# Neighbourhood attention on one core: the order, the loads and the sends of the closing projection

## The chip, the cores and the metric

The kernel runs on one core of one Trainium2 chip. The metric is the device time of one execution in microseconds. Three executions of the kernel before took 1041.56, 1041.59 and 1039.85 us; their median, 1041.56 us, is the number that the change is measured against.

## What is computed

One encoder layer (DEPTH is 1) with neighbourhood attention over 2048 tokens of width 1024, 16 heads of width 64, all in float32:

```python
h = rmsnorm(x, norm_0)
q, k, v, gate = jnp.split(h @ w_in_0, 4, axis=-1)
o = neighbourhood_attention(heads(q), heads(k), heads(v), rpb_0)
x = x + (o * jax.nn.silu(gate)) @ w_out_0
return rmsnorm(x, norm_f)
```

The change touches the last two lines alone: the product with `w_out_0` (1024 by 1024), the addition of the rows of `x`, the final norm, and when the operands of these arrive.

## The kernel before, in words

**Stages.** `stage_one` and `stage_two` compute q, k, v and the gate. Then a loop of 33 steps (m = 0 to 32) runs the attention, one pair of heads and one quarter T of the tokens a step: scores (L972), the bias added from a table tile `em` (L981), exponentials, transposes (`turns`, L1015), and the product with the values (`values`, L1034), whose result is multiplied by the gate tile `sgt` (L1038, tile `og`) and stored to DRAM as `ogd`. Between these parts `feed(n)` weaves in n matmuls of other work, first the remaining values, then `outputs()` (L1229 to L1233), which is the output projection of the first 1024 tokens. In the first half of the tokens the projection is a plain product; a finished row is stored by L1142.

**The end stretch.** The second 1024 tokens are projected by `tail()`, after the loop. They form four units n = 0 to 3 of 256 tokens. Each unit is a 2 by 2 block product done with seven block products P = 1 to 7 (a Strassen form) in place of eight. A product is 12 matmuls (L1304): 4 slices of the inner dimension, each with three matmuls, because every float32 operand is split into a high and a low part. Left operands are the four blocks A11, A12 (loaded by `load_a`, L1267), A21, A22 (`load_b`, L1276), or the sums S1 to S4 of them (`sum_a`, VectorE, L1289); each is split by `form_a` into the two parts, ScalarE first (L436), then VectorE (L437), into a tile `f`. Right operands are three blocks of the weights, which lie in SBUF, and four combinations T1 to T4, which stage two had formed and stored to DRAM as `wodT`; each has 4 slices of 2 parts, so 32 loads of 256 KB in all bring them back (`load_w`, L1416).

**Which product waits for which.** The products of one unit share three PSUM banks: P 1 and 2 one, P 6, 7 and 4 the second, P 5 and 3 the third. A bank keeps accumulating: `evac_o` reads it after P 6 (L1371, L1372: U2 = bank + U1, then added to the row), and only then may P 7 add to it; it is read again after 7 (L1375, L1376) before 4 may go on. L1362 and L1363 belong to P 2, L1379 to P 5, L1383 to P 4, L1389 to P 3. After P 4 and after P 3 a row block is complete: ScalarE squares it (L1315), VectorE and ScalarE make the root (L1321 to L1323), VectorE scales both halves (L1328), and `send` stores them (L1332). The very last block has its own code, `last_row` (from L1343 on), with its two stores at L1354.

**What sets the order.** `order_t` is the order of the 28 products, written by hand. Every other instruction of the end stretch is put in a list with a due time counted in matmuls (`at`, `store`), and `due` emits what has come due after each matmul. Emission fixes the order inside each engine and inside each queue: an instruction that waits holds all behind it on its engine. All loads and all but one store go out on one queue, SyncE's (SP). Forms come due 23 matmuls before their product, the root of a row 6 matmuls after its last addition, its scaling 12 and its send 24 after.

**Tiles.** `get2` hands out 128 by 512 tiles: the free list `free2` first, else a new tile from a pool named by the list `grow`. A new tile takes the slot whose content is the oldest of its pool, and its first writer waits until that content has been read; for `raw` these are finished rows of the first half, waiting for L1142. `places` lists the slots for the combinations, made of tiles that the attention no longer needs.

Of the kernel before, what the change touches and what calls it, by code (L numbers as in the profile page):

```python
# [60 lines left out]
def build(ctx, tc, x, xr, xt, wg, tab, w_out, n0, nf, out):  # L61
# [1188 lines left out]
    def get2():  # L1250
        if not free2:
            return grow.pop(0)([128, 512], F32, "t2")
        return free2.pop(0)
# [3 lines left out]
    order_t = [(0, 1), (1, 1), (0, 2), (1, 2), (2, 1),  # L1257
# [4 lines left out]

# [54 lines left out]
    def finish_o(n, a):  # L1317
# [12 lines left out]
        def send():  # L1330
            for c in range(2):
                nc.sync.dma_start(out[row(n, a):row(n, a) + 128, 512 * c:512 * c + 512], R[n, a, c])  # L1332
                free2.append(R[n, a, c])
# [22 lines left out]
    def evac_o(n, P):  # L1356
# [16 lines left out]
        elif P == 7:  # L1373
            U[n, 3] = U[n, 2]
            nc.vector.tensor_tensor(U[n, 3], p, U[n, 1], OP.add)  # L1375
            nc.vector.tensor_tensor(R[n, 1, 1], R[n, 1, 1], U[n, 3], OP.add)  # L1376
            free2.append(U[n, 1])
        elif P == 5:
            nc.vector.tensor_tensor(R[n, 1, 1], p, R[n, 1, 1], OP.add)  # L1379
            square_o(n, 1, 1)  # L1380
            free2.append(U[n, 3])
        elif P == 4:
            nc.vector.tensor_tensor(R[n, 1, 0], p, R[n, 1, 0], OP.add)  # L1383
            square_o(n, 1, 0)
            finish_o(n, 1)
        elif (n, P) == (3, 3):
            last_row()
        else:
            nc.vector.tensor_tensor(R[n, 0, 1], p, R[n, 0, 1], OP.add)  # L1389
            square_o(n, 0, 1)  # L1390
            finish_o(n, 0)

    def before_end(m):
        if m == cycles - 1:
            load_b(0, [ep([128, 512], F32, "og2") for _ in range(2)])
            load_a(0, wp([128, 1024], F32, "og4"))

    def tail():
        for k in range(4):
            for f, q, j in (("B11", k, 0), ("B21", 4 + k, 0), ("B22", 4 + k, 1)):  # L1400
                WO[f, k] = woh[q, j], wol[q, j]
        load_a(1, wp([128, 1024], F32, "og4"))
        places = places_of([(emp, 4), (kp, 2), (emp, 4), (kp, 2)] + sixths() + [(vp, 2)] * 2 + [(mkp, 3)])
        places = list(places) + [qp([128, 512], F32R, "tw") for _ in range(2)] + [xp([128, 512], F32R, "tw") for _ in range(7)]
        grow.extend([sp] * 2 + [raw] * 4 + [ev] * 4 + [rbp] * 3 + [ev] * 2 + [raw] * 2 + [xp, lp])
        base = 576 - fed[0]
        slots_ = {u: base + 12 * i for i, u in enumerate(order_t)}

        def at(t, f, *a):
            store(("tail",), t, lambda: f(*a))  # L1410

        def load_w(f, k):
            WO[f, k] = places.pop(0), places.pop(0)
            must(*[("wo", k, f, m) for m in range(2)])
            for m in range(2):
                nc.sync.dma_start(WO[f, k][m].bitcast(F32), wod[f][:, k, m])  # L1416

# [5 lines left out]
        for n in range(4):  # L1423
# [3 lines left out]
            if n > 1:  # L1427
                at(14 if n == 2 else base + 72, load_a, n)
            if n:
# [5 lines left out]
            for P in range(1, 8):  # L1435
                at(max(at_[P] - 23, 1), form_and_free, n, P)
        for f, t in (("T2", 1), ("T3", 20), ("T1", 36), ("T4", 52)):
            for k in range(4):
                at(t + 3 * k, load_w, f, k)
        while next(outs, 0) != 0:  # L1440
            due(1)
        for n, P in order_t:
# [63 lines left out]
    for m in range(cycles + 1):  # L1506
        a = amount[m] - 6
        begin(m)
        feed(6)
        if m:  # L1510
# [3 lines left out]
        if m:  # L1514
            for k in range(4):
                if not split_rows() and k % 2:
                    consume(1, turn=True)
                feed(a * (0.17, 0.17, 0.17, 0.19)[k])
# [53 lines left out]
```

## Time and profile before

| | us |
|---|---|
| median of three executions | 1041.56 |
| the profiled execution's own time | 1039.36 |
| its span | 1037.6 |
| TensorE busy in the span | 1010.8 (97%) |
| VectorE, ScalarE, GpSimd busy | 708.9, 517.7, 161.6 |
| last matmul of the first half's projection starts | 930.60 |
| first matmul of the end stretch starts | 930.83 |
| last matmul of the end stretch starts | 1028.87 |

All times of the trace are counted from the start of the span. A row of the timeline gives start, duration, engine, line, operation, `out<-in` and shape; what stands in brackets is how long the engine stood idle before the row and what released it. "PEclk" is the granted share of TensorE's clock.

### The profile page before, as it was taken

What the parts mean: (1) busy time and instruction counts of PE and PEld (TensorE: products, weight loads), DVE (VectorE), ACT (ScalarE), POOL (GpSimd) and SP (SyncE); (2) the same over time, 40 slices, a digit from 0 to 9 for tenths busy, and PEclk for the clock granted to TensorE, in tenths of its full rate; (3) what the DMA queues carried; (4) which work ended last, traced back from release to release, by engine and by line L of the source; (5) the groups of instructions that cost most, each with busy time, mean ns of one, the idle gap of its engine ahead of it and who ended that gap; (6) DMA issues with size and microseconds to landing.
All of it is one profiled execution on the core that took longest, in us unless ns stands there. A gap on an engine that the chain in (4) does not pass through costs nothing.

```text
span 1037.6 us, 21699 instructions
## 1 busy us (share of the span) xinstructions
PE 1010.8 (97%) x8128; PEld 813.4 (78%) x8128; DVE 708.9 (68%) x1569; ACT 517.7 (50%) x1301; POOL 161.6 (16%) x277
## 2 busy tenths in 40 slices
PE   9999999999999999999999999999999999996896
PEld 6888888887888888888888877777777777785774
DVE  5476657678897896767675656667667676653775
ACT  7645323244234443424333357787777776742333
POOL 0000231221221400000000022232332322310000
PEclk9999999999999999999999999999999999998899
DMA  9633444452735344665753798999888989879322
GB/s 318 230 102 102 142 144 134 129 160 85 202 102 183 99 136 156 219 195 165 218 178 111 239 271 284 317 338 316 267 279 267 312 292 329 295 232 391 124 99 82
DMA packets 125442, 213.84 MB, mean 206 GB/s; under 512 B 11352, under 2 KB 45528, under 8 KB 125336
## 3 DMA queue, kind: packets, MB, share of 16 engines
q1 hardware_dynamic: 124904, 212.05, 63.5%
q8 instruction: 64, 1.05, 0.4%
q10 hardware_dynamic: 432, 0.40, 0.1%
q14 instruction: 42, 0.34, 0.1%
HBM read 153.69 MB, written 58.72 MB: 205 GB/s over the span
## 4 chain that ended last, share of the span: by engine, by line
PE 81%; DVE 9%; DMA 3%; ACT 3%; issue 2%; SPq 1%; POOL 0%; DVEq 0%; ACTq 0%
PE pp L354 41%; PE pv L478 8%; PE o L1034 7%; PE s L972 6%; PE pv L871 4%; PE ph L1015 4%; PE po L1233 3%; PE po L1229 3%; PE po L1231 3%; PE pt L1304 2%; DMA kt<-kd 1%; DVE f L437 1%; DVE l L437 1%; DMA out_dram<-y 1%; DVE t L1328 1%
## 5 line engine op out<-in xcount | busy, mean ns | idle before, releaser
L354 PE MATMUL pp<-h,f 128*128 128x512 f32 x768 | 248.4, 389 | 0.0
L354 PEld LDWEIGHTS pp<-h,f 128*128 128x128 f32 x768 | 144.2, 188 | 29.8
L354 PE MATMUL pp<-four,f 128*128 128x512 f32 x648 | 160.8, 389 | 0.4 <-DVE u L367 0.3
L354 PE MATMUL pp<-l,f 128*128 128x512 f32 x384 | 149.4, 389 | 0.0
L354 PEld LDWEIGHTS pp<-four,f 128*128 128x128 f32 x648 | 121.4, 188 | 26.5 <-DVE u L367 1.4
L986 ACT ACTIVATE x<-x,st 128x264 f32<-128x264 f32 (+1 forms) x256 | 124.4, 487 | 23.8 <-DVE st L981 23.8
L998 POOL TENSOR_SCALAR x<-x,st 128x264 f32<-128x264 f32 (+1 forms) x192 | 86.9, 470 | 236.7 <-DVE st L991 236.0
L374 POOL TENSOR_TENSOR tmp<-tmp,rb 128x512 f32<-128x512 f32 x36 | 59.2, 1647 | 268.1 <-DVE tmp L372 223.4
L981 DVE CUSTOM_DVE_ANT_0 x<-s,em 128x264 f32<-128x264 f32 (+1 forms) x256 | 89.5, 404 | 2.0 <-PE s L972 1.8
L1034 PEld LDWEIGHTS o<-pta,vt 120*64 120x64 f32 (+2 forms) x1024 | 68.5, 137 | 19.8 <-DVE st L981 12.2
L354 PEld LDWEIGHTS pp<-l,f 128*128 128x128 f32 x384 | 72.1, 188 | 15.0
L1034 PE MATMUL o<-pta,vt 120*64 120x192 f32 (+5 forms) x1024 | 83.4, 316 | 0.0
L1018 DVE COPY pta<-ph 120x512 f32<-120x512 f32 (+5 forms) x96 | 56.0, 637 | 39.4 <-PE ph L1015 39.3
L362 ACT ACTIVATE p<-pp 128x512 f32<-128x512 f32 x24 | 14.3, 597 | 122.6 <-PE pp L354 122.6
L437 DVE TENSOR_TENSOR f<-raw,f 128x512 fp32r<-128x512 f32 x80 | 55.0, 690 | 27.1 <-ACT f L436 27.1
L1018 ACT ACTIVATE pta<-ph 120x512 f32<-120x512 f32 (+5 forms) x96 | 49.1, 557 | 41.7 <-PE ph L1015 41.7
L972 PE MATMUL s<-kt,qt 64*32 64x264 f32 (+1 forms) x2048 | 67.1, 374 | 0.6 <-DVE pta L1018 0.4
L436 ACT ACTIVATE f<-raw 128x512 fp32r<-128x512 f32 x80 | 49.5, 625 | 32.3 <-PE pp L354 16.6
L478 PE MATMUL pv<-wh,h 128*128 128x512 f32 x192 | 63.7, 392 | 0.4 <-ACT h L439 0.4
L478 PE MATMUL pv<-wl,h 128*128 128x512 f32 x192 | 63.4, 390 | 0.0
L478 PE MATMUL pv<-wh,l 128*128 128x512 f32 x192 | 63.2, 389 | 0.0
L372 DVE TENSOR_TENSOR tmp<-pp,u 128x512 f32<-128x512 f32 x48 | 33.1, 689 | 40.1 <-PE pp L354 35.4
(207 smaller groups left out, 1770.9 us busy)
## 6 DMA issues: line engine op xcount, KB each, us to landing
raw<-in_wg_dram SPq DMA_DIRECT2D x124, 256.0 KB, 4.3
em<-in_tab_dram SPq DMA_DIRECT2D x16, 912.0 KB, 7.5
em<-in_tab_dram SPq DMA_DIRECT2D x16, 528.0 KB, 7.4
vd<-v SPq DMA_DIRECT2D x32, 256.0 KB, 2.7
sgd<-sg SPq DMA_DIRECT2D x32, 256.0 KB, 3.7
qt<-qd SPq DMA_DIRECT2D x32, 256.0 KB, 5.7
sgt<-sgd SPq DMA_DIRECT2D x32, 256.0 KB, 8.4
ogd<-og SPq DMA_DIRECT2D x32, 256.0 KB, 3.8
```

Source lines behind the costliest of these rows:

```text
L354: nc.tensor.matmul(B[n, P], t[:, int(m == 2), c], x[k][int(m == 1)], start=P in (1, 6, 5) and k == 0 and m == 0, stop=k == 3 and m == 2, s ...
L374: nc.gpsimd.tensor_tensor(tmp, tmp, rb[c], OP.mult)
L436: nc.scalar.activation(h, t, AF.Copy)
L437: nc.vector.tensor_tensor(l, t, h.bitcast(F32), OP.subtract)
L478: nc.tensor.matmul(ps[t], a[:, o], b, start=k == 0 and m == 0, stop=k == NK - 1 and m == 2)
L871: nc.tensor.matmul(p, x_[:, o], w_, start=k == 0 and m == 0, stop=k == NK - 1 and m == 2)
L972: nc.tensor.matmul(pst[s][h * 32:h * 32 + 32], qt[e, q:q + 32], keys.rearrange("p r (s c) -> p s r c", c=8), start=True, stop=True)
L981: nc.vector.tensor_tensor_reduce(X[i, C][s], ps, em, -1.0, 1e38, OP.add, OP.min, st[:, o:o + 1])
L986: nc.scalar.activation(X[i, C][s], X[i, C][s], AF.Exp, bias=st[:, o:o + 1], scale=-1.0, accum_out=st[:, 4 + o:5 + o])
L998: nc.gpsimd.tensor_scalar(X[i, C][s], X[i, C][s], st[:, o:o + 1], 1.0, op0=OP.mult, op1=OP.mult)
L1018: (nc.vector.tensor_copy if h else lambda o, i_: nc.scalar.activation(o, i_, AF.Copy))(to[:k, :, 2 - j, h, c], at[h][:k, :, c])
L1034: nc.tensor.matmul(o[s * 64:s * 64 + 64, g0 * 64:g1 * 64 + 64].rearrange("d (g q) -> d g q", q=64), vt[:k, strip, s * 64:s * 64 + 64], t[: ...
```

## The change

- **Order.** `order_t` is rearranged. Between two products of one bank there now stand two products of other banks, and P 5 may run ahead of P 7; the reading of the bank after P 5 then waits, in the program, for that after P 7 (`waits`).
- **Loads.** T2 and T1 are no longer loaded in `tail`. Half of T2 is loaded in the step before the last, ahead of that step's scores; the other half, the operand block of unit 1 and all of T1 are loaded at the start of the last step, ahead of the last gate tile. T3 comes due at 2 (was 20) and T4 at 40 (was 52). The second operand blocks of unit 1 (`load_b(1)`) come due by the same rule, 90 before (1, 6), which the new order puts at 9 (was 69).
- **Sends.** The stores of L1332 go out from GpSimd's queue in place of SP's.
- **Tiles.** Other slots for the combinations; and once the first half's projection has ended, `get2` takes new tiles first and freed ones after.
- **Steps from 10 on.** `split_rows` and `consume`, which split operands of the first half's projection, are tried in the first two of four places of a step in place of all four (`consume` in two of four before, too).

```diff
     def get2():
-        if not free2:
+        if not free2 or grow and fed[0] >= 576:
             return grow.pop(0)([128, 512], F32, "t2")
         return free2.pop(0)
...
     order_t = [(0, 1), (1, 1), (0, 2), (1, 2), (2, 1),
-               (0, 6), (2, 2), (0, 7), (0, 5), (0, 4), (0, 3),
-               (1, 6), (3, 1), (1, 7), (1, 5), (1, 4), (1, 3),
-               (2, 6), (3, 2), (2, 7), (2, 5), (2, 4), (3, 6), (2, 3),
-               (3, 7), (3, 5), (3, 4), (3, 3)]
+               (0, 6), (1, 6), (0, 5), (0, 7), (1, 5), (1, 7), (0, 4), (0, 3),
+               (3, 1), (2, 2), (1, 4), (1, 3), (3, 2),
+               (2, 6), (3, 6), (2, 5), (2, 7), (3, 5), (3, 7), (2, 4), (2, 3), (3, 4), (3, 3)]
+    waits = {}
...
         def send():
             for c in range(2):
-                nc.sync.dma_start(out[row(n, a):row(n, a) + 128, 512 * c:512 * c + 512], R[n, a, c])
+                nc.gpsimd.dma_start(out[row(n, a):row(n, a) + 128, 512 * c:512 * c + 512], R[n, a, c])
                 free2.append(R[n, a, c])
...
             free2.append(U[n, 1])
+            waits.pop(n, lambda: None)()
+        elif P == 5 and (n, 3) not in U:
+            waits[n] = lambda: evac_o(n, 5)
         elif P == 5:
...
     def before_end(m):
         if m == cycles - 1:
             load_b(0, [ep([128, 512], F32, "og2") for _ in range(2)])
             load_a(0, wp([128, 1024], F32, "og4"))
+            places.extend(list(places_of([(mkp, 3), (lp, 1)])))
+            for k in range(2):
+                load_w("T2", k)
+
+    def last_begin():
+        places.extend(list(places_of([(emp, 4), (kp, 2), (emp, 4), (kp, 2)])))
+        for k in range(2, 4):
+            load_w("T2", k)
+        load_a(1, wp([128, 1024], F32, "og4"))
+        for k in range(4):
+            load_w("T1", k)
...
     def tail():
...
-        load_a(1, wp([128, 1024], F32, "og4"))
-        places = places_of([(emp, 4), (kp, 2), (emp, 4), (kp, 2)] + sixths() + [(vp, 2)] * 2 + [(mkp, 3)])
-        places = list(places) + [qp([128, 512], F32R, "tw") for _ in range(2)] + [xp([128, 512], F32R, "tw") for _ in range(7)]
-        grow.extend([sp] * 2 + [raw] * 4 + [ev] * 4 + [rbp] * 3 + [ev] * 2 + [raw] * 2 + [xp, lp])
+        places.extend(sixths() + list(places_of([(vp, 2)] * 2)) + [qp([128, 512], F32R, "tw") for _ in range(2)]
+                      + [xp([128, 512], F32R, "tw") for _ in range(4)])
+        grow.extend([sp] * 2 + [raw] * 4 + [ev] * 4 + [rbp] * 3 + [ev] * 2 + [raw] * 2 + [xp] * 4)
...
             if n > 1:
-                at(14 if n == 2 else base + 72, load_a, n)
+                at(24 if n == 2 else base + 100, load_a, n)
...
-        for f, t in (("T2", 1), ("T3", 20), ("T1", 36), ("T4", 52)):
+        for f, t in (("T3", 2), ("T4", 40)):
             for k in range(4):
                 at(t + 3 * k, load_w, f, k)
         while next(outs, 0) != 0:
+            fed[0] += 1
             due(1)
...
         begin(m)
+        if m == cycles:
+            last_begin()
         feed(6)
...
             for k in range(4):
-                if not split_rows() and k % 2:
+                if m < 10 and not split_rows() and k % 2 or m >= 10 and k < 2 and not split_rows():
                     consume(1, turn=True)
```

More of the change, by code (lines that the diff above doesn't have):

```diff
@@ L1391, in evac_o, with load_w @@
             finish_o(n, 0)
+    places = []
+    def load_w(f, k):
+        WO[f, k] = places.pop(0), places.pop(0)
+        must(*[("wo", k, f, m) for m in range(2)])
+        for m in range(2):
+            nc.sync.dma_start(WO[f, k][m].bitcast(F32), wod[f][:, k, m])
     def before_end(m):
@@ L1410, in at @@
             store(("tail",), t, lambda: f(*a))
[L1412 to L1416, printed above, removed]
         def form_and_free(n, P):
```

## The prediction, made before the change had run

> **What bounds the kernel now.** I read first the page, then the waits of TensorE, then its timeline in the end stretch, then what held it there.
>
> ```profile
> span 1037.6 us, 21699 instructions
> PE   9999999999999999999999999999999999996896
> PEclk9999999999999999999999999999999999998899
> ```
>
> TensorE is the bound, except in the last slices. From 280 to 930 us its waits come to two rows:
>
> ```profile
> PE s L972 <- DVE pta L1018: 0.4, 1, 0.4
> PE pp L354 <- DVE u L367: 0.3, 1, 0.3
> ```
>
> So 0.7 us is all that the loop could win, and the change can pay only in the end stretch. TensorE's timeline there, with the idle time in brackets:
>
> ```profile
> 930.83 0.39 PE L1304 MATMUL pt<-woh,f 128*128 128x512 f32 x1
> ...
> 949.64 0.39 PE L1304 MATMUL pt<-woh,f 128*128 128x512 f32 x1
> 960.54 2.90 PE L1304 MATMUL pt<-four,f 128*128 128x512 f32 x6 [10.51 <-issue]
> ...
> 981.05 2.60 PE L1304 MATMUL pt<-four,f 128*128 128x512 f32 x6 [2.13 <-DVE t L1371]
> ...
> 1001.34 2.44 PE L1304 MATMUL pt<-four,f 128*128 128x512 f32 x6 [2.08 <-DVE t L1371]
> ...
> 1016.97 1.62 PE L1304 MATMUL pt<-four,f 128*128 128x512 f32 x6 [0.18 <-DVE t L1371]
> ...
> 1028.87 0.39 PE L1304 MATMUL pt<-woh,f 128*128 128x512 f32 x1
> ```
>
> The first 7 products (84 matmuls, 930.83 to 949.64) run unhindered at 18.81 / 83 = 0.2266 us a matmul, 2.72 us a product. At that pace the last of 336 would start at 930.83 + 335 x 0.2266 = 1006.8. It starts at 1028.87: **22.1 us are lost**, and four rows, all before a P 7, hold most of it. Each is followed by a slow stretch of 36 matmuls, which at 0.2266 would take 8.16 us:
>
> ```profile
> 949.87:960.54 10.67, 0.16 (x2) 0.03 (x1) 1.36 (x3) 0.00 (x0) 0.00 (x0) 0.70 1.05 401
> 960.54:970.60 10.06, 10.06 (x36) 8.16 (x37) 7.85 (x13) 3.12 (x7) 0.00 (x0) 0.81 0.30 97
> 981.05:990.93 9.88, 9.88 (x36) 8.01 (x37) 6.87 (x11) 3.00 (x6) 0.00 (x0) 0.83 0.58 192
> 1001.34:1011.19 9.85, 9.85 (x37) 7.97 (x37) 7.88 (x14) 3.12 (x7) 0.00 (x0) 0.83 0.17 58
> 1016.97:1026.38 9.41, 8.56 (x36) 6.75 (x37) 6.50 (x11) 2.90 (x8) 0.00 (x0) 1.00 0.24 91
> ```
>
> (Columns: stretch, length, busy time of TensorE, its weight loads, VectorE, ScalarE, GpSimd; granted clock, DMA share, GB/s.) Idle and slow: 10.51 + 1.90, 2.13 + 1.72, 2.08 + 1.69, 0.18 + 1.25, together 21.5; the rest is 4 x 0.16, since a matmul's modelled 0.39 us reach past the pace. A stop of 2.1 us costs 1.7 us more through the clock (0.83); one of 0.18 does not (1.00).
>
> The Trainium skill, "TensorE: Matmul & The Clock Gate", section "What's actually happening", has the clock halved after an idle window of about 3.4 us. By that rule a 2.1 us stop would cost no clock; the trace disagrees, and goes by.
>
> **What ends the 10.51 us** is on VectorE and on SP's queue:
>
> ```profile
> 959.15 0.69 DVE L1289 TENSOR_TENSOR og<-t,t 128x512 f32<-128x512 f32 x1 [12.68 <-DMA t<-ogd]
> 959.75 0.68 DVE L1371 TENSOR_TENSOR t<-pt,t 128x512 f32<-128x512 f32 x1
> 953.16 0.97 SPq L1276 DMA_DIRECT2D t<-ogd  x2
> 955.20 0.98 SPq L1142 DMA_DIRECT2D out_dram<-y  x2
> ```
>
> VectorE stands 12.68 us at the sum S1 of unit 1, whose operands SP issued only at 953.16, behind 32 loads of combinations. Behind that sum on VectorE stands L1371, the reading of the bank that (0, 7) needs. The DMA share is 1.05: the queue is full, not idle.
>
> **The change part by part.**
>
> *Order and early loads: 22.1 us at stake.* T1 and T2, 16 loads, leave the end stretch, and `load_b(1)` comes due at 9 of 27 matmuls ahead of the first product. Ahead of it on SP stand then six loads of T3 and one store; with its own two that is 9 x 0.262 MB = 2.36 MB, or 5.9 us at the 401 GB/s above. From 925 on (the first T3 slot is free when the values' product ends, at 924.7) that makes 931, and 2 to 3 us later they have landed (first row of the view of issues; the last number is us from issue to landing):
>
> ```profile
> t<-ogd SPq DMA_DIRECT2D x6, 256.0 KB, 3.4
> sgt<-sgd SPq DMA_DIRECT2D x4, 256.0 KB, 8.0
> out_dram<-y SPq DMA_DIRECT2D x7, 256.0 KB, 5.3
> ```
>
> S1(1) comes due 39 matmuls in, at 933.5. It is late by nothing to 1 us, and (0, 6), the first in need of what stands behind it, starts at 944.4; I take +0.5 with 0 and 2 as ends. The three other stalls go too: two products, 5.4 us, now cover the 2.1 us of reading the bank. So all 22.1 us go, and VectorE is next.
>
> *What VectorE gives back in the middle.* The sums of units 2 and 3 come due 60 to 30 matmuls ahead of (2, 6) and (3, 6), which now stand side by side (places 19 and 20 of 28; before 18 and 23). The four rows of units 0 and 1 are finished in (0, 4), (0, 3), (1, 4), (1, 3), at places 12 to 17. All this falls into the 8 products from (0, 3) to (3, 6), 21.8 us of TensorE. VectorE has there, in its order from the addition after (0, 4) to the form of (2, 5): 7 forms, 8 sums, 8 additions, 8 scalings, 4 roots. Prices:
>
> ```profile
> 970.86 0.68 DVE L1383 TENSOR_TENSOR t<-pt,t 128x512 f32<-128x512 f32 x1
> 972.92 0.69 DVE L437 TENSOR_TENSOR f<-t,f 128x512 fp32r<-128x512 f32 x1 [1.37 <-ACT f L436]
> 973.53 0.21 DVE L1321 TENSOR_SCALAR st<-st 128x1 f32<-128x1 f32 x1
> 974.24 1.41 DVE L1328 SCALAR_TENSOR_TENSOR t<-t,st,acc 128x512 f32<-128x512 f32 x2 [0.51 <-ACT st L1323]
> 975.57 0.68 DVE L1389 TENSOR_TENSOR t<-pt,t 128x512 f32<-128x512 f32 x1
> ...
> 1026.58 0.69 DVE L1383 TENSOR_TENSOR t<-pt,t 128x512 f32<-128x512 f32 x1 [1.26 <-PE pt L1304]
> 1028.12 0.22 DVE L1321 TENSOR_SCALAR st<-st 128x1 f32<-128x1 f32 x1 [0.85 <-ACT t L1315]
> 1028.84 1.42 DVE L1328 SCALAR_TENSOR_TENSOR t<-t,st,acc 128x512 f32<-128x512 f32 x2 [0.51 <-ACT st L1323]
> 1030.17 0.74 DVE L1343 TENSOR_TENSOR t<-pt,t 128x256 f32<-128x256 f32 x2
> L437 DVE TENSOR_TENSOR f<-t,f 128x512 fp32r<-128x512 f32 x16 | 11.0, 689 | 13.1 <-ACT f L436 13.1
> ```
>
> Full tiles start 0.60 us apart (972.92 to 973.53), two scalings take 1.33. An addition with its row's end takes 4.71 us when a form lies between (970.86 to 975.57), 3.59 without (1026.58 to 1030.17). Less the tiles in it, a root costs 2.18 or 1.66 us of standing. So 23 x 0.60 + 4 x 1.33 + 4 x 1.66 = 25.8 us at least; with 2.18, 27.8; and if the three forms that don't lie in such a chain wait for ScalarE like those of the last row above, 13.1 / 16 = 0.82 us each, 30.3. TensorE falls behind by 4.0 to 8.5 us. I take **+7.5**, since 16 forms waited. A slow clock inside adds nothing, VectorE sets the pace there.
>
> *What it gives back at the end.* After (2, 4) come (2, 3), (3, 4), (3, 3): three rows end in three products, and the last row stands behind their chains on VectorE: 4.71 + 3.59 + 3.59 = 11.9 us. The last matmul starts 8.16 us after that of (2, 4); the additions start some 0.7 us after a matmul's start (0.39 and a hand-over). So the last row begins 12.6 - 8.2 = 4.4 us after the last matmul's start, in place of 1030.17 - 1028.87 = 1.3; up to 0.6 more if the form ahead is late: 3.1 to 3.7, taken **+3.4**.
>
> *Sends from GpSimd.* SP no longer stands behind scalings. At the very end two sends follow the last row's:
>
> ```profile
> 1032.64 0.33 SPq L1354 DMA_DIRECT2D out_dram<-og  x1
> 1033.02 0.92 SPq L1332 DMA_DIRECT2D out_dram<-t  x2
> L374 POOL TENSOR_TENSOR tmp<-tmp,rb 128x512 f32<-128x512 f32 x36 | 59.2, 1647 | 268.1 <-DVE tmp L372 223.4
> ```
>
> They can now go 1.3 us sooner at best (1032.64 to 1033.94). No row shows a send from GpSimd; its nearest are SP's 0.33 to 0.46 us and GpSimd's costliest tile, 1.65 us. At 1.65 the last six end after 4.71 + 9.9 = 14.6 us from the addition after (2, 4), and the last row's own stores go at 11.9 + 2.5 (1030.17 to 1032.64) = 14.4: hidden. Taken **-0.5**, ends -1.3 and 0. One new wait hangs on a send: S2 of unit 3 is written into a tile that the send of row (0, 1) empties, with all of VectorE's queue behind it. Between that row's scaling and S2 lie 6 tiles, 2 scalings and a root, 6 x 0.60 + 1.33 + 2.18 = 7.1 us, against 1.65 + 5.3 (a store's landing, above) = 7.0: nothing lost.
>
> *Early loads in the last two steps.* Ahead of the last gate tile SP now has the 16 loads of T1 and T2 and the operand block of unit 1 (0.52 MB): 4.7 MB, 11.7 us at 401 GB/s.
>
> ```profile
> 910.26 0.49 SPq L922 DMA_DIRECT2D sgt<-sgd  x1
> 924.69 0.69 DVE L1038 TENSOR_TENSOR og<-o,sgt 128x512 f32<-128x512 f32 x1 [3.25 <-PE o L1034]
> ...
> 926.18 0.68 DVE L437 TENSOR_TENSOR f<-og,f 128x512 fp32r<-128x512 f32 x1
> ```
>
> The tile was issued at 910.26; with 8.0 us to landing (row above) and a queue already full it would land at 930.0. VectorE wanted it at 924.7; the first form ends 2.2 us after (926.86) and is needed at 930.8, so 4.0 us are slack, and 1.3 us are lost. If the queue has gaps there that the loads fill, nothing is. Taken **+0.4**, ends 0 and 1.3. *Steps from 10 on:* TensorE waits 0.7 us in them; two splits a step move by half a step. Nothing, from -0.7 to +1.
>
> **Sum:** -22.1 + 0.5 + 7.5 + 3.4 - 0.5 + 0.4 = **-10.8 us**. The profiled execution took 1039.36 us (span 1037.6, 1.8 around it), 2.2 below the median of 1041.56; it would take 1028.6, and the median 1041.56 - 10.8 = **1030.8**. With all ends: -22.1 + 0 + 4.0 + 3.1 - 1.3 - 0.7 = -17.0 to -22.1 + 2 + 8.5 + 3.7 + 0 + 1.3 + 1 = -5.6: 1024.6 to 1036.0.
>
> **The rivals.**
>
> 1. *Loads still late.* If the early loads move at three quarters of 401 GB/s, the gate tile, T3 and `load_b(1)` slip together. The 4.7 MB take 15.6 us, the gate tile lands at 933.9, 9.2 late, 5.2 beyond the slack: a gain of 10.8 + 0.4 - 5.2 = 6.0, time 1035.6; a little slower still, 1037. For it: DMA shares of 1.05 say that the queue can be full. Against it: the 401 GB/s were moved with the very same kind of load. Chance 0.13.
> 2. *VectorE hides all.* If roots and forms stand for nothing because later tiles fill the gaps, 7.5 falls to 0 and 3.4 halves: -10.8 - 7.5 - 1.7 = -20.0, 1021.6. Against: VectorE keeps its order, and 13.1 us of standing are in the trace. Chance 0.07.
> 3. *The same wait by another door.* The new tile for U1 of unit 2 is the slot of the last row that L1142 sends. If that store leaves at 955.20 as before, ScalarE holds there from 944.4 to 960.5 (5.3 us to landing) and the form of (0, 5) is 12 us late: -10.8 + 12 = +1.2, 1042.8, so the change would not do what it says. Against: 16 loads, 4.2 MB or 10.5 us at 401, no longer stand ahead of it. Chance 0.05.
> 4. *Slower: GpSimd's sends.* If a send waits for VectorE or costs more than a tile, the last six are the end. Beyond 1.65 us each adds sixfold; the gain is used up at 1.65 + 10.8 / 6 = 3.45 us a send. At 2.5 times the row of L374, 4.1 us, it is 6 x 2.45 = 14.7: +3.9, 1045.5. For it: VectorE is almost without pause in those chains. Against: they stand 1.7 to 2.2 us at each root. Chance 0.07.
>
> The Trainium skill, "SBUF — State Buffer", section "A bandwidth-pool intuition that's wrong", speaks for rival 4: while VectorE runs in a two-port mode GpSimd can't write its descriptors, and such a DMA took 3.1 us in place of 0.62. By that figure the sixfold excess would be 8.7 us and the time an estimated 1039.5. The same page, "Who interferes with whom", gives `tensor_tensor` no such mode; no row of before shows a send beside it.
>
> **How the numbers follow.** The forecast has 0.68. The range reaches down to rival 2's side and up to rival 1's: 1024.5 to 1037. What a measurement can tell here is 0.2%, 2.1 us (1039.5 to 1043.6). Faster: 0.68 + 0.13 + 0.07 = 0.88; same: rival 3, 0.05; slower: rival 4, 0.07.
>
> **What would show it.** Right: no idle before (0, 7); the clock near 1.00 until place 12; VectorE without a pause of over 2.5 us from there to (2, 5), with stops of TensorE of 0.5 to 3 us; the last row's first piece 4 to 5 us after the last matmul's start. Wrong: a DMA as releaser of VectorE or ScalarE for over 2 us; the gate tile landing after 931; sends on GpSimd's queue over 3 us; stops of over 5 us anywhere.

## The result and the profile after

| | before, us | after, us |
|---|---|---|
| median | 1041.57 (1039.85 to 1042.11) | 1033.87 (1033.24 to 1034.67) |
| profiled execution: time, span | 1039.36, 1037.6 | 1034.67, 1032.9 |
| end stretch's first matmul, last matmul | 930.83, 1028.87 | 932.03, 1021.10 |
| last row's first piece | 1030.17 | 1026.53 |

The kernel before ran once more beside the changed one, hence its median of 1041.57. The ratio of after to before is 0.9929, with a 95% interval of 0.9912 to 0.9946: 7.7 us faster between the medians. Between the two profiled executions it is 4.7 us, because that of before lies 2.2 us below its median and that of after 0.8 above. The working below goes by the profiled ones.

The head of the page after, and its slices of TensorE's busy share and granted clock:

```profile
span 1032.9 us, 21696 instructions
PE   9999999999999999999999999999999999998985
PEclk9999999999999999999999999999999999999998
```

The slices with a low clock are gone but for the last one. TensorE's waits from 280 to 930 us came to 0.7 us; after:

```profile
PE s L972 <- DMA kt<-kd: 1.2, 2, 0.8
...
PE s L972 <- issue: 0.2, 1, 0.2
```

These two are new, and small; those of before are there as they were. TensorE's timeline in the end stretch, the rows with stops (one of 0.22 us left out) and those from which the distances below are taken:

```profile
932.03 0.39 PE L1304 MATMUL pt<-woh,f 128*128 128x512 f32 x1
...
940.51 0.79 PE L1304 MATMUL pt<-woh,f 128*128 128x512 f32 x1 [2.88 <-ACT t L1360]
...
950.21 8.96 PE L1304 MATMUL pt<-four,f 128*128 128x512 f32 x36
...
985.28 0.50 PE L1304 MATMUL pt<-woh,f 128*128 128x512 f32 x1 [0.51 <-ACT f L436]
...
989.27 3.33 PE L1304 MATMUL pt<-four,f 128*128 128x512 f32 x12 [0.70 <-ACT f L436]
...
994.52 7.93 PE L1304 MATMUL pt<-four,f 128*128 128x512 f32 x24 [1.92 <-ACT f L436]
...
1002.29 2.20 PE L1304 MATMUL pt<-sixths,f 128*128 128x512 f32 x9
...
1021.10 0.39 PE L1304 MATMUL pt<-woh,f 128*128 128x512 f32 x1
```

None of the four stops before a P 7 is left, the 10.51 us least of all. 950.21 is the start of (0, 6), the sixth product, and 1002.29 that of (2, 7), the 22nd. At 0.2266 us a matmul they would stand 13.60 us after the first one and 43.51 us after each other. So there is a lag of 4.6 us up to (0, 6) (18.18 - 13.60), one of 8.6 us from there to (2, 7) (52.08 - 43.51), and none behind: 18.81 us for the last 83 steps, the bare pace. What it did to the end shows on VectorE:

```profile
1019.48 0.68 DVE L1392 TENSOR_TENSOR t<-pt,t 128x512 f32<-128x512 f32 x1
...
1024.48 0.21 DVE L1321 TENSOR_SCALAR st<-st 128x1 f32<-128x1 f32 x1 [0.79 <-ACT t L1315]
...
1026.53 0.75 DVE L1343 TENSOR_TENSOR t<-pt,t 128x256 f32<-128x256 f32 x2
```

Each of the two additions (L1392 of (2, 3), L1386 of (3, 4)) is followed by its root and its scalings, with waits of 0.79 and 0.50 us for ScalarE, 3.5 us a row; the last row stands behind both. It begins 5.43 us after the last matmul (1026.53 - 1021.10), in place of 1.30. From there the span has 6.37 us to run, in place of 7.43. The ledger: start of the stretch +1.2, stalls -22.1, lag to (0, 6) +4.6, lag to (2, 7) +8.6, last row +4.1, end -1.1: together -4.7, the difference of the spans. Of the 22.1 us gained, 17.3 were given back in the first six products, in the middle and at the end; the other 1.2 lie ahead of the stretch. They are there by the first matmul of the first half's projection (699.7 us in place of 698.4), and 0.6 of them by the first scores of the loop (599.7 in place of 599.1), ahead of everything that the change touches.

### The profile page after: what moved, and what is told of

It reads as the page before. It is cut to its first block, busy times and chain, and to the rows that moved or that the text cites. A ratio compares the mean times of both kernels' runs of the same rounds, so it can differ in the third digit from the quotient of the medians.

```text
span 1032.9 us, 21696 instructions
## 1 busy us (share of the span) xinstructions
PE 1010.2 (98%) x8128; PEld 810.8 (78%) x8128; DVE 709.0 (69%) x1569; ACT 516.4 (50%) x1301; POOL 169.3 (16%) x291
## 4 chain that ended last, share of the span: by engine, by line
PE 79%; DVE 9%; DMA 7%; ACT 3%; issue 2%; SPq 1%; POOL 0%; DVEq 0%; ACTq 0%
PE pp L354 41%; PE pv L478 8%; PE o L1034 7%; PE s L972 5%; PE pt L1304 4%; PE ph L1015 4%; DMA kt<-kd 3%; PE pv L871 2%; PE po L1233 2%; PE po L1231 2%; PE po L1229 2%; DMA four<-wodT 1%; DMA vt<-vd 1%; DVE l L437 1%; DVE t L1328 1%
```

## The experiments

Each was timed beside the kernel before, whose medians there were 1040.5 to 1041.6. In some of them line numbers are shifted by a few. "After" is the changed kernel, 1033.87. The interval of its ratio (0.9912 to 0.9946) overlaps those of the runs within 3 us of it; for these the profile has to show where the time went.

### The loads and the first six products

**The gate tile first.** In after SP issues, ahead of the gate tile, 16 loads of combinations, 0.68 to 0.76 us each:

```profile
910.11 6.05 SPq L1402 DMA_DIRECT2D four<-wodT  x8
...
917.81 5.40 SPq L1402 DMA_DIRECT2D four<-wodT  x8
923.53 0.32 SPq L922 DMA_DIRECT2D sgt<-sgd  x1
...
930.65 0.53 SPq L1041 DMA_DIRECT2D ogd<-og  x1
...
933.34 0.90 SPq L1276 DMA_DIRECT2D t<-ogd  x2
```

VectorE then stands 7.33 us for that tile, and later 1.81 us for the last load of the list, `load_b(1)`, which had stood behind the store of the last `og` and four loads of T3:

```profile
929.93 0.69 DVE L1038 TENSOR_TENSOR og<-o,sgt 128x512 f32<-128x512 f32 x1 [7.33 <-DMA sgt<-sgd]
...
938.68 0.69 DVE L1289 TENSOR_TENSOR t<-t,t 128x512 f32<-128x512 f32 x1 [1.81 <-DMA t<-ogd]
```

```diff
         if m == cycles:
+            all_loads()
             last_begin()
```

> The changed kernel, with the last gate tile's load put ahead of the loads of the last step (the other half of T2, T1 and the operand block of unit 1). Theory A (VectorE's wait of 7.33 us for that tile is what makes TensorE start the end stretch's third product late, 4.6 us in all by the pace): 1033.9 - 4.6 = 1029.3 us, between 1028.5 and 1030.5; the wait on the gate tile gone, no stop at (0, 2). Rival B (the queue is full either way, so the combinations just come later): a stop of 3 to 5 us at (0, 6) or (0, 5) instead, 1033 to 1035 us.

It took 1030.91 us, ratio 0.9903 (0.9888 to 0.9918), 3.0 less than after. The wait for the gate tile was gone, and the lag to (0, 6) 1.9 us in place of 4.6. The stop before (0, 2) was 1.58 in place of 2.88, since `load_b(1)` was still late: VectorE stood 3.25 us for it. The mechanism holds, but 1030.91 lies 0.4 above theory A's range and the stop did not go; the rest of the lag belongs to `load_b(1)`.

**All loads late again.** After with all 32 loads of combinations, and `load_a(1)`, back in the end stretch.

```diff
         if m == cycles - 1:
...
-            for k in range(2):
-                load_w("T2", k)
...
-        for k in range(2, 4):
-            load_w("T2", k)
...
-        for k in range(4):
-            load_w("T1", k)
...
     def tail():
...
+        last_begin()
...
-        for f, t in (("T3", 2), ("T4", 40)):
+        for f, t in (("T2", 1), ("T1", 20), ("T3", 36), ("T4", 52)):
```

> The changed kernel with all 32 loads of combinations and the operand block of unit 1 back in the end stretch (T2 due at 1, T1 at 20, T3 at 36, T4 at 52); order, sends and tiles as changed. Theory A (load_b(1) ahead of most loads is what ended the long stop; the early loads themselves only delay the gate tile): 1033.9 - 4.6 = 1029.3, up to 2 more if T3 or T4 come late: 1028.5 to 1031.5. Rival B (the early loads carry the gain): TensorE waits for combinations at (0, 5) or (0, 7), 4 to 8 us, 1036 to 1040.

It took 1041.50 us, ratio 0.9999 (0.9986 to 1.0012): the whole gain gone. Neither expectation held: TensorE stopped 6.91 us before (0, 5), for a form, and ScalarE shows why that was late:

```profile
958.39 0.60 ACT L1360 ACTIVATE t<-pt 128x512 f32<-128x512 f32 x1 [9.08 <-issue]
```

L1360 writes U1 of unit 2 into its new tile, and that tile's slot held the last finished row of the first half until L1142, queued behind the loads, had sent it:

```profile
952.61 0.96 SPq L1142 DMA_DIRECT2D out_dram<-y  x2
```

This was still only read from the trace, so the next run changed the slot alone.

```diff
-        grow.extend([sp] * 2 + [raw] * 4 + [ev] * 4 + [rbp] * 3 + [ev] * 2 + [raw] * 2 + [xp] * 4)
+        grow.extend([sp] * 2 + [raw] * 4 + [ev] * 4 + [rbp] * 3 + [ev] * 2 + [raw] + [xp] * 4 + [raw])
```

> e3_late_loads with one edit: the list of slots that the end stretch takes its tiles from has its last two kinds swapped, so that the first sum tile of unit 2 (U1) no longer takes the slot of the row y of n=7, whose send lands at 958 in e3. All 32 loads stay late. Theory A (that slot is why the changed kernel with late loads loses all: U1's copy waited 9.08 there, the forms queued behind it, product (0,5) stopped 6.91): the stop goes, 1034.6 = 1041.5 - 6.9, between 1033 and 1036. Theory B (the late loads themselves set the time; the stop is only moved to load_a(2), which landed late too, 5.43): 1039.5 to 1041.5.

1032.33 us, ratio 0.9911 (0.9898 to 0.9925): 9.2 us for one slot (the tiles handed out after it move up by one), and no slower than after with its early loads. ScalarE's row for the same tile has no wait any more:

```profile
951.63 0.58 ACT L1360 ACTIVATE t<-pt 128x512 f32<-128x512 f32 x1
```

So theory A's cause holds, and the time is even 0.7 us under its range. More follows: with the new order and this slot the early loads are not needed. That order brings `load_b(1)` forward, by its rule, and no stop before (0, 7) is left without them.

### The order of the products

**The old order, all else as after.**

```diff
-               (0, 6), (1, 6), (0, 5), (0, 7), (1, 5), (1, 7), (0, 4), (0, 3),
...
+               (0, 6), (2, 2), (0, 7), (0, 5), (0, 4), (0, 3),
...
```

> The changed kernel with the order of products of before, all else (early loads, sends from GpSimd, tiles) as changed. Theory A (the 12.6 us at the first (0, 7) were late loads, the three later stops the old order; the new order gives back 8.6 in the middle and 4.1 - 1.3 more at the end): the first stop gone, the stops of about 2 us at (1, 7) and (2, 7) there again, no stretch with VectorE behind; 1033.9 + 9.5 - 8.6 - 4.1 = 1030.7, between 1029 and 1033. Rival B (the new order is where the gain is): 1038 or more.

1032.71 us, ratio 0.9917 (0.9902 to 0.9932), theory A's number. The old order with the new loads, tiles and sends is as fast as the new one. Its first long stop is 4.13 us in place of 10.51, and the two of some 2 us before a P 7 are still there (L1372 there is L1371):

```profile
956.20 3.64 PE L1305 MATMUL pt<-sixths,f 128*128 128x512 f32 x9 [4.13 <-issue]
976.59 3.69 PE L1305 MATMUL pt<-sixths,f 128*128 128x512 f32 x9 [2.47 <-DVE og L1372]
996.68 3.63 PE L1305 MATMUL pt<-sixths,f 128*128 128x512 f32 x8 [2.08 <-DVE t L1372]
```

Two remedies for one stall don't add up: early loads take most of it, the new order takes it too. And the 4.13 us left are not all late loads. `load_b(1)` went out by 947.95, and the slowest load of its line took 5.0 us to landing, so it was there by 953.0; VectorE's sum started later and was released by a store of the first half:

```profile
954.80 0.69 DVE L1290 TENSOR_TENSOR t<-t,t 128x512 f32<-128x512 f32 x1 [4.57 <-DMA out_dram<-y]
```

L1290 is L1289 elsewhere. By that row the new list of tiles gave its result, too, a slot that L1142 had still to empty. The old order with another slot there was not tried. I thought then that the remaining stops showed the worth of the order. That fell as well, below.

### The middle: amount or order on VectorE

**Forms three matmuls earlier.**

```diff
-                at(max(at_[P] - 23, 1), form_and_free, n, P)
+                at(max(at_[P] - 26, 1), form_and_free, n, P)
```

> The changed kernel with forms due 26 matmuls ahead of their product in place of 23, so that ScalarE's half of a form stands ahead of the square of the row just added, not behind it. Theory A (the 8.6 us in the middle are VectorE standing 1.3 to 1.4 us for ScalarE after each row's last addition): stops of TensorE between (0, 3) and (2, 5) fall by 3 to 7 us, 1033.9 - 5 = 1029, between 1027 and 1031. Rival B (VectorE has too many tiles there, whoever stands first): less than 1 us, 1033 to 1034.5.

1032.70 us, ratio 0.9911 (0.9894 to 0.9927). The lag in the middle fell from 8.6 to 5.4. That is neither theory. Forms now come due ahead of the addition, but nothing stands between an addition and its root, so VectorE waits there for the square (in each of the seven roots; together 5.1 us):

```profile
980.30 0.21 DVE L1321 TENSOR_SCALAR st<-st 128x1 f32<-128x1 f32 x1 [0.79 <-ACT t L1315]
```

Its waits for ScalarE's half of a form were not gone either, as the edit had meant: they fell from 13.2 to 9.3 us, since some of these halves still stand behind a square or a root. I read the run as speaking for the amount of work, and tested that.

**Eight sums on GpSimd.** All of units 2 and 3, so 5.5 us of VectorE's tiles.

```diff
-        nc.vector.tensor_tensor(A[n, f], A[n, a], A[n, b], o)
+        (nc.gpsimd if n > 1 else nc.vector).tensor_tensor(A[n, f], A[n, a], A[n, b], o)
```

> The changed kernel with the eight sums of units 2 and 3 (S1 to S4 of the left factor) taken from VectorE to GpSimd: 8 x 0.685 = 5.5 us less on VectorE between 970 and 1000; on GpSimd a sum of this shape took 1.64 us earlier in the run, 13.1 in all. Theory A (in the middle of the end stretch VectorE has more tiles than product time, and that is the 8.6 us by which (2,7) is late): the lag falls to about 3 to 4, time 1029 to 1030. Theory B (the lag comes from the order on VectorE, operations that wait for ScalarE's squares and forms and hold up those behind, not from the amount): 1032.5 to 1034. Theory C (GpSimd's sums come too late or slow VectorE's own operations beside them): 1034 or more, with stops released by a sum, or VectorE's 128x512 sums well over 0.69 us.

1032.26 us, ratio 0.9909 (0.9895 to 0.9922); lag in the middle 6.1. That is 2.5 us for 5.5 us of work taken away: neither theory. Some of the 5.5 came back: beside GpSimd's sums two forms took 0.90 and 1.27 us in place of 0.69, and two pairs of scalings 1.73 in place of 1.41, 1.4 us in all. What was left had one shape. These are rows of VectorE and then of ScalarE in after, around one product:

```profile
987.20 0.68 DVE L1386 TENSOR_TENSOR t<-pt,t 128x512 f32<-128x512 f32 x1
989.25 0.69 DVE L437 TENSOR_TENSOR f<-t,f 128x512 fp32r<-128x512 f32 x1 [1.37 <-ACT f L436]
```

```profile
987.98 0.63 ACT L1315 ACTIVATE t<-t 128x512 f32<-128x512 f32 x1 [2.75 <-DVE t L1386]
...
988.61 0.61 ACT L436 ACTIVATE f<-t 128x512 fp32r<-128x512 f32 x1
```

Ahead of that square ScalarE stood idle for 2.75 us. In its queue the square of the row stands ahead of the next form, and the square needs VectorE's addition (987.20). Only then comes the form (988.61), and VectorE, whose next entry is the second half of that form, stands 1.37 us. Addition, square, form, form: a round trip through ScalarE at each of these products, and the next product's form, needed at 989.27, is ready just then.

**The square later.** It comes due three matmuls after the addition, and so stands behind the form in ScalarE's queue. VectorE's order is unchanged.

```diff
-        nc.scalar.activation(junk[0], R[n, a, c], AF.Square, ...)
+        def square():
+            nc.scalar.activation(junk[0], R[n, a, c], AF.Square, ...)
+        if (n, a, c) == (3, 0, 0):
+            square()
+        else:
+            store(("y", n, a), 3, square)
```

> The changed kernel with the squares of the end stretch (all but one) put three matmuls later, so that on ScalarE the high part of the next form stands ahead of the square of the row just added, and no longer behind it. In the changed kernel each evacuation that has a square makes a round trip: VectorE adds the row, ScalarE squares it, only then rounds the form, and VectorE stands still 1.31 to 1.37 for that form with the next evacuation behind it. Theory A (this round trip is the lag in the middle): the waits DVE f for ACT f of 1.3 us fall to under 0.7, the stops between 980 and 1000 go, 4 to 7 us saved, 1027 to 1030. Theory B (the number of tiles on VectorE sets it; its waits are only moved to the roots, that stand behind later squares): 1032 to 1034. The half-way result of the run with the sums on GpSimd (1032.3) speaks for A.

1024.81 us, ratio 0.9841 (0.9828 to 0.9855): 9.1 us less than after, more than theory A had allowed. VectorE's waits for ScalarE's half of a form, from 960 to 1029 us (total, count, longest), in before, in after and here:

```profile
DVE f L437 <- ACT f L436: 13.9, 12, 1.4
```

```profile
DVE f L437 <- ACT f L436: 13.2, 11, 1.4
```

```profile
DVE f L437 <- ACT f L436: 1.8, 3, 0.7
```

VectorE is busy for 27.40 of 30 us from 970 to 1000, so it had nearly too much to do, but just not too much. The prediction's own prices say so too: without the roots' standing its 23 tiles and 4 pairs of scalings come to 19.1 us, against 21.8 of TensorE. The lag in the middle is 1.4 us, TensorE's only stop in it 0.33. The last row begins 2.91 us after the last matmul in place of 5.43, since VectorE is less far behind. By the profiles: stretch 0.6 earlier, middle -7.2, first six products +0.4, last row -2.5, together -9.9, the difference of the spans (1023.0 and 1032.9).

**The old order with the square later.** The edit of the old order and the one above, together.

```diff
-               (0, 6), (1, 6), (0, 5), (0, 7), (1, 5), (1, 7), (0, 4), (0, 3),
...
+               (0, 6), (2, 2), (0, 7), (0, 5), (0, 4), (0, 3),
...
+            store(("y", n, a), 3, square)
```

> The run with the old order of products (1032.7, as fast as the new order, 1033.9), now with the squares three matmuls later as well; with the new order that took 9.1 us off (1024.8). Theory A (the new order does remove the stops between products of one bank, and the round trips through ScalarE had eaten that gain): in the old order the stops before each P 7 (2.47, 2.08 and what the clock loses after them) stay, since they are the reading of the bank and not a form; 1029 to 1033, so that the new order is worth 5 to 8 once the squares are out of the way. Theory B (the order is worth nothing, the round trips cost the same in both): 1023 to 1026.

1025.73 us, ratio 0.9856 (0.9836 to 0.9876), against 0.9841 (0.9828 to 0.9855) with the new order: theory B, not to be told apart. VectorE's waits for ScalarE's halves of forms fell from 13.2 us (old order, squares as they were) to 1.2. TensorE's stops from the first long one on:

```profile
954.47 3.72 PE L1305 MATMUL pt<-sixths,f 128*128 128x512 f32 x9 [4.24 <-issue]
972.96 2.32 PE L1305 MATMUL pt<-sixths,f 128*128 128x512 f32 x9 [0.45 <-DVE og L1379]
995.74 0.93 PE L1305 MATMUL pt<-four,f 128*128 128x512 f32 x3 [0.65 <-DVE t L1383]
```

Lines of this run are shifted: L1379 is L1371, the reading of the bank ahead of a P 7, and L1383 is L1375, the one ahead of a P 4. So of the stops of 2.47 and 2.08 us before a P 7 one is left with 0.45 and the other is gone. They were not the price of reading a bank. One product, 2.72 us, covers that but for the 0.45. They were the same round trips, which had made VectorE late for the reading. The first long stop stays (4.24 us), with the same store as releaser of the sum. So the order is worth nothing only on balance: up to the last matmul the new order is 2.6 us less behind the pace, and its last row begins 1.6 us later after it (2.91 against 1.29).

The kernel before shows the same, but only in its trace, since the squares alone were not moved there. Ahead of the stop of 2.13 us at 981.05 VectorE waits for forms three times (the prediction shows one, at 972.92), each time behind a row's square, and comes to the reading of the bank, L1371, at 980.23:

```profile
977.57 0.69 DVE L437 TENSOR_TENSOR f<-t,f 128x512 fp32r<-128x512 f32 x1 [1.31 <-ACT f L436]
...
980.23 0.68 DVE L1371 TENSOR_TENSOR t<-pt,t 128x512 f32<-128x512 f32 x1
```

### Sends and steps

**Sends from SP again.**

```diff
-                nc.gpsimd.dma_start(out[row(n, a):row(n, a) + 128, 512 * c:512 * c + 512], R[n, a, c])
+                nc.sync.dma_start(out[row(n, a):row(n, a) + 128, 512 * c:512 * c + 512], R[n, a, c])
```

> The changed kernel with the finished rows of the end stretch sent from SyncE's queue again. Theory A (the sends are worth about what the end of the span showed, -1.1 between the start of the last row and the end, and hinder nothing before): 1034.9, between 1034.2 and 1035.2. Theory B (worth nothing, the end differs by run variation): 1033.9. Theory C (a send that waits for its scaling on SyncE's queue holds up loads queued behind it, A of unit 3 and residual rows among them, and the new order needs these on time): 1037 or more, with PE stops released by forms or sums behind a DMA.

1035.41 us, ratio 0.9940 (0.9928 to 0.9953). The medians say 1.5 us, but the interval overlaps with that of after. The place is in the profile: from the last row's first piece to the end of the span 7.4 us (1026.69 to 1034.1), in after 6.37, since two sends follow the last row's own on SP again:

```profile
1029.16 0.33 SPq L1354 DMA_DIRECT2D out_dram<-t  x1
1029.55 0.42 SPq L1332 DMA_DIRECT2D out_dram<-og  x1
1030.02 0.45 SPq L1332 DMA_DIRECT2D out_dram<-t  x1
```

Theory A by the place, with a time 0.2 above its range. TensorE's stops have the releasers that they have in after, and none is a DMA.

**The steps from 10 on as before.**

```diff
-                if m < 10 and not split_rows() and k % 2 or m >= 10 and k < 2 and not split_rows():
+                if not split_rows() and k % 2:
```

> The changed kernel with the edit of the steps from the tenth on undone (transposes' consumers and row splitting in their old places). Theory A (it does nothing that counts; the end stretch's start at 932.03 beside 930.83 is variation at the start of the run): 1033.9, between 1033.2 and 1034.6, end stretch's first matmul within 1 us of 932. Theory B (the edit is why the stretch starts 1.2 later): 1032.7. Theory C (the edit is needed to have rows split and K transposes ready on time): 1035 or more, with new PE stops between 700 and 930.

1035.25 us, ratio 0.9934 (0.9920 to 0.9948): not to be told from after, though above theory A's range. Theory B is out: the stretch began at 931.71, within 0.4 us. So is C's reason: the longest wait of TensorE between 280 and 930 us is 0.5 us. In the profile the run is 1.5 us longer by its lag to (0, 6), 6.4 in place of 4.6, which varies between runs (below).

### Together

The squares later, the gate tile first, `load_b(1)` at the start of the end stretch into two `raw` tiles, and U1 of unit 2 out of that slot:

```diff
+        load_b(1, [raw([128, 512], F32, "t2") for _ in range(2)])
+        grow.extend([sp] * 2 + [raw] * 2 + [ev] * 4 + [rbp] * 3 + [ev] * 2 + [raw] + [xp] * 4 + [raw])
...
-            if n:
+            if n > 1:
                 at(at_[6] - 90, lambda n=n: load_b(n, [get2() for _ in range(2)]))
```

> The squares later, as in the run of that alone; the gate tile of the last step loaded ahead of the weights; the second half of unit 1's rows (load_b of unit 1) issued at the start of the end stretch ahead of the late loads, into two slots of their own; and the first sum tile of unit 2 kept out of the slot of the row y of n=7. Theory A (each of the named causes adds up): 3.0 less for the gate tile, up to 2 less for the stop at product (0,2), 4 to 7 less in the middle: 1022 to 1026. Theory B (the causes are in series behind one another, and what one frees the next takes): 1028 to 1031.

1019.57 us, ratio 0.9793 (0.9780 to 0.9806), better than theory A: 22 us under the kernel before. One stop of TensorE is left in the end stretch, and the page shows a full row but for the end:

```profile
987.54 3.33 PE L1304 MATMUL pt<-four,f 128*128 128x512 f32 x12 [0.32 <-ACT f L436]
```

```profile
PE   9999999999999999999999999999999999999996
PEclk9999999999999999999999999999999999999998
```

The same with the eight sums on GpSimd as well:

```diff
-        nc.vector.tensor_tensor(A[n, f], A[n, a], A[n, b], o)
+        (nc.gpsimd if n > 1 else nc.vector).tensor_tensor(A[n, f], A[n, a], A[n, b], o)
```

> The same as the run of all together, with the eight sums of units 2 and 3 on GpSimd as well. Theory A (with the round trips gone VectorE has room, and the sums are hidden there): no different from the run without, within 0.5. Theory B (VectorE's amount still bounds the middle): 1.5 to 3 less. Theory C (GpSimd's sums of 1.3 to 1.8 us each now come too late for the forms): 1 to 3 more.

1022.72 us, ratio 0.9832 (0.9811 to 0.9853): 3.1 us more, theory C by its number, but not by its reason. GpSimd's sums slow VectorE beside them. A row of GpSimd, then rows of VectorE:

```profile
977.91 2.99 POOL L1289 TENSOR_TENSOR t<-t,t 128x512 f32<-128x512 f32 x2 [1.71 <-DVE f L437]
```

```profile
977.69 0.67 DVE L1393 TENSOR_TENSOR t<-pt,t 128x512 f32<-128x512 f32 x1
978.29 1.46 DVE L437 TENSOR_TENSOR f<-t,f 128x512 fp32r<-128x512 f32 x1
...
980.38 2.77 DVE L1335 SCALAR_TENSOR_TENSOR t<-t,st,acc 128x512 f32<-128x512 f32 x2 [0.51 <-ACT st L1330]
```

The form took 1.46 us in place of 0.69 and two scalings 2.77 in place of 1.41. The addition from PSUM, which reads one operand from SBUF, kept its 0.67; in the earlier run with these sums one lay wholly beside a sum (962.95 to 963.64, the sum from 962.32 to 964.07) and took 0.69. The Trainium skill, "SBUF — State Buffer", section "Who interferes with whom", says that a VectorE instruction with two SBUF inputs contends with a GpSimd instruction that reads SBUF; the trace agrees. Between the two profiled executions, 2.0 us apart, 1.2 us lie in the middle. Another 1.0 lie behind the last row's first piece, where the last two stores took 3.2 and 3.4 us to land in place of 2.0 and 2.4; the sums were long done by then, and the cause of that is open.

A table of the runs that bear on the middle, by the distances defined above, in us:

| | median | lag to (0, 6) | lag to (2, 7) | last row after last matmul |
|---|---|---|---|---|
| after | 1033.87 | 4.6 | 8.6 | 5.43 |
| gate tile first | 1030.91 | 1.9 | 8.7 | 5.43 |
| forms three earlier | 1032.70 | 9.2 | 5.4 | 4.30 |
| sums on GpSimd | 1032.26 | 5.1 | 6.1 | 5.43 |
| square later | 1024.81 | 5.0 | 1.4 | 2.91 |
| together | 1019.57 | 0.7 | 1.2 | 2.91 |

The forms' run had in its profile a longer wait for the gate tile (9.73 us), which in that execution took back what the middle had gained. The lag to (0, 6) varies between runs that hardly differ up to there: 4.6 in after, 5.0 and 5.1 with the square later and the sums on GpSimd, 6.9 with the sends from SP.

## Why the prediction was right, and where it was wrong

- *The 22.1 us of stalls go.* Right as a sum: no stop before a P 7 is left. Half of the reason was wrong. That early loads and an early `load_b(1)` end the 10.51 us holds, and each alone does most of it (4.13 us left with the one, part of it a slot; nothing with the other, given the other slot). But "two products, 5.4 us, now cover the 2.1 us of reading the bank" took a wait's releaser for its cause. L1371 released TensorE, but L1371 was late because VectorE stood in round trips before it; with these gone the old order stops before a P 7 once more for 0.45 us, behind its first long stop.
- *Loads, +0.5 and +0.4.* This is the term that was mis-sized most: +4.6. The gate tile, issued at 923.53, reached VectorE at 929.93, as predicted (930.0). What I missed hangs on that. The store of the last `og` waits for it on SP, and `load_b(1)` stands behind that store, so it went out at 933.34 and not at 931. Its sum then held VectorE for 1.81 us; behind the sum stands a root of the first half, and behind that root, on ScalarE, the copy out of the bank that (0, 2) adds to:

```profile
939.53 0.20 ACT L1133 ACTIVATE st<-st 128x1 f32<-128x1 f32 x1 [3.10 <-DVE st L1132]
...
939.88 0.58 ACT L1360 ACTIVATE t<-pt 128x512 f32<-128x512 f32 x1
```

  So TensorE stopped for 2.88 us at 940.51, and with the slow clock after it (0.51 over the next 3.1 us) that made most of the 4.6. The prediction had taken (0, 6) for the first product in need of what stands behind that sum; it was (0, 2). It is not rival 1: the loads moved as fast as forecast, and what slipped stood behind a store that waited. Putting the gate tile first took 3.0 us off.
- *VectorE in the middle, +7.5.* Measured 8.6, just beyond my upper end of 8.5. The size was right for a wrong reason, because I took the standing of 1.66 to 2.18 us a root, and of 0.82 a form, from the rows of before as if it belonged to the work. It belonged to the order of square and form on ScalarE. The row that says so, 13.1 us of VectorE standing for ScalarE's halves of forms, was in my own fence.
- *End, +3.4.* Measured +4.1, by the same chain; with the square later it is 1.6 (2.91 - 1.30).
- *Sends, -0.5.* The end is 1.1 us shorter, within the ends given. A send took 0.54 to 0.65 us on GpSimd, so rival 4 had no part, and the 3.1 us that the Trainium skill, "SBUF — State Buffer", section "A bandwidth-pool intuition that's wrong", gives for a hindered one didn't show beside VectorE's additions and scalings:

```profile
975.95 1.29 POOL L1332 DMA_DIRECT2D out_dram<-t  x2 [59.38 <-DVE t L1328]
...
1026.91 0.54 POOL L1332 DMA_DIRECT2D out_dram<-t  x1
```

- *Steps from 10 on, nothing.* The runs don't contradict it.
- *The signs.* No idle before (0, 7), the gate tile before 931, no stop of over 5 us and stops of 0.5 to 2 us in the middle came as the prediction had them. Three did not: the clock fell to 0.51 after the stop at (0, 2), the last row began 5.43 us after the last matmul's start and not 4 to 5, and a DMA released VectorE after 7.33 us and ScalarE after 3.94 (945.40), a sign of being wrong.
- *Rival 2*, VectorE hides all, did not come, though one edit brings it about. *Rival 3*, the same wait by another door, was the mechanism of the run with late loads: 9.2 us hang on one slot, and in after it is only covered. The sum there left the time as it was before, as the rival had said.

So -10.8 was forecast and -7.7 measured, -4.7 by the profiles, from which the terms were read. That the medians stand nearer to the forecast than the profiles is the scatter of the executions, and luck; the sum failed by the lag up to (0, 6), +3.7, with +1.1 in the middle, +0.7 and -0.6 at the end and +1.2 ahead of the stretch. Open stays what an earlier `load_b(1)`, or the squares later, would have done in the kernel before by itself, and whether the old order, with every other remedy of the run of all together, would be as fast as that; none of these was tried.

## What to carry to other kernels

When an engine's timeline shows a wait, ask of the releaser what it had waited for, and go on until you come to work or to a queue's order; a chain "addition, square, form, form" over two engines costs its whole length at each turn as long as the later form stands behind the square, and moving one instruction past another in the idle engine's queue can be worth more than rearranging the matmuls (here 9.1 us, where the order was worth nothing on balance). Two remedies for one stall don't add up, so undo each alone before crediting either. A tile that takes over a slot waits for the slot's last reader, here a store at the end of a full queue: look up for each new tile when that reader is done.

## What the runs showed of the hardware

The granted clock after a stop of nearly the same length was not always the same. After the stop of 1.92 us in after it was 0.78 over the next 7.8 us; after one of 1.96 us at the same product, in the run with late loads and the other slot, 1.00 (length, busy times, then clock, DMA share, GB/s):

```profile
994.50:1002.30 7.80, 7.78 (x25) 5.42 (x26) 6.70 (x13) 2.73 (x8) 1.08 (x2) 0.78 0.20 80
```

```profile
993.20:997.85 4.65, 3.29 (x13) 2.10 (x13) 3.59 (x8) 1.70 (x6) 1.08 (x2) 1.00 0.27 112
```

In that run TensorE then stopped once more, 1.35 us, and reached (2, 7) 7.78 us after that product's start, in after 7.77: VectorE set the pace, and the clock cost nothing there. The very same stop of 1.96 us was followed by 0.78 in the runs with the gate tile first, with late loads and with the steps as before, and by 1.00 in the run with the sends from SP.

Where the clock did fall it was near a half for some 3.4 us, and nearly full after that: in after 0.54 from 994.50 to 997.90 and 0.97 from there to 1002.30; in the kernel before, behind the stop of 10.51 us, 0.50 from 960.54 to 964.00 and 0.98 from there to 970.60.
